# First stage of a two-layer diffusion backbone in another order: modulation blocks ahead of the token tiles' norms

## The chip, the cores and the metric

The program runs on one core of a Trainium2 chip. The metric is the device time of one execution in microseconds (us); the figure compared is the median over runs. The engines are TensorE (PE; PEld is its weight load), VectorE (DVE), ScalarE (ACT), GpSimd (POOL) and SyncE (SP), which issues nearly all transfers here. Each engine works through its own instructions strictly in the order in which they are written, and starts one when the semaphores it names have arrived.

## What is computed

```python
def layer(x, cond, s0_h, s0_r, pos, p):
    mod = jax.nn.silu(cond) @ p["ada_w"] + p["ada_b"]
    sh_m, sc_m, g_m, sh_f, sc_f, g_f = ...            # six vectors of 1024
    h = rmsnorm(x, p["norm_mix"]) * (1.0 + sc_m) + sh_m
    y, S_a, S_b = token_mixers(h, p, s0_h, s0_r, pos)  # h @ w_in, recurrences, @ w_out
    x = x + g_m * y
    h = rmsnorm(x, p["norm_ffn"]) * (1.0 + sc_f) + sh_f
    gate, up = jnp.split(h @ p["w_up"], 2, axis=-1)
    return x + g_f * ((jax.nn.silu(gate) * up) @ p["w_down"]), S_a, S_b
```

Two such layers run over 128 context tokens (condition `c_ctx`) and 512 latent tokens (condition `c`), all in float32, and a last norm follows. Matters here: before the first product with `w_in`, the first layer's scale and shift (2048 of the 6144 columns of `ada_w`) have to be known, and the five tiles of 128 tokens normed.

## The kernel before

The 640 tokens are five tiles `t` of 128 (tile 0 is the context). Products with big weights are made in split passes: an operand `f` is cut into `hi = fp32r(f)` (a cast on ACT) and `lo = f - hi` (a subtraction on DVE), and PE sums hi\*hi + hi\*lo + lo\*hi. The weights come through `Stream` (`W`): `load` issues a transfer of 512 KB on SP's queue, `cut` (L75 on ACT, L76 on DVE) makes `wh` and `wl`. Four `wh`/`wl` pairs and three `raw` buffers exist.

The first stage is `ada_first` (L318 on). It is written under a manual schedule: each engine's order is the order of the calls. Its pieces:

- Block `i` (0 to 3) is 512 columns of `ada_w`: 0 and 1 are the scale and the shift of features 0 to 511, 2 and 3 those of features 512 to 1023. `load(i)` issues four transfers of 512 KB (quarters `j`). `cut(i, j)` makes a quarter's hi (L343, ACT) and lo (L344, DVE). `mm(i, j0, j1)` multiplies quarters with the two silu'd conditions: for blocks in `FAST` four matmuls of 512 columns a quarter, hi and lo alternating (L354), for the others plain float32 matmuls (L357), which need no cut. After quarter 3 ACT copies the sum out (`row`, L362). `rt(i)` turns it into columns (L368, four small matmuls in eight passes), and `fin(i)` adds the bias (L375, DVE; L378 for scales).
- Token tile `t`: `sq` sums squares (L548, ACT; then `rstd`: L559 on DVE and a power on POOL, L561), `xs` scales (L387, DVE), `tr` transposes eight 128x128 squares on PE (L567) and `xc` copies them out (L394, ACT). `full(t, hf)` applies scale and shift to half `hf` of the features, two squares on DVE (L409) and two on ACT (L407), except that `kd=4` puts all on DVE; `split(t, hf)` makes hi (L413, ACT) and lo (L414, DVE) in `hT`.
- The list `out` mixes such calls with entries `(u, hf, k0, k1)`: unit `u` (zf, zb, qa of the first head) for features `k0` to `k1` in eighths, and token half `hf`: 0 is tiles 0 and 1 (256 columns), 1 the other three (384 columns). An entry is 12 matmuls (L605 to L607). The six entries with `4, 8` need the features of blocks 2 and 3; they end the stage. They start with tiles 0 and 1, then go on to the others.
- `setup_lb` (L227 on) computes, from `cols`, the lower bounds of the gates: three small DVE operations, a power of 16 columns on POOL (L236), and eleven small DVE operations (`setup_lb2`). The gates that ACT evaluates when a unit is done (L698) need it.

After the stage the rest of the two layers follows: PE works through `w_in`, `w_out`, `w_up` and `w_down`, while lanes of other work (scans, later modulation, tables) are stepped in between by a count of written-out costs.

Of the kernel before, what the change touches and what calls it, by code (L numbers as in the profile page):

```python
# [20 lines left out]
NT = 5  # L21
# [20 lines left out]
ACC1 = -25.0  # L42
Q_TAB = 2.6
KD = 2
FAST = (0, 1, 3)
CUT = 256
Q_SCAN = 2.65
Q_ADA = (3.0, 2.0, 4.0)
# [54 lines left out]
class Net:  # L103
# [217 lines left out]
    def ada_first(self):  # L321
# [4 lines left out]
        def load(i):  # L326
            col = (1 - i % 2) * 1024 + (i // 2) * 512
            for j in range(4):
                w = self.B("adw")
                nc.sync.dma_start(out=w[:, :1024].rearrange("p (k n) -> p k n", k=2),  # L330
                                  in_=a["ada_w"][0, 2 * j * P:(2 * j + 2) * P, col:col + 512].rearrange(
                                      "(k p) n -> p k n", p=P))
                raws.append(w)
        pr, pc, row, cuts = {}, {}, {}, {}

        def cut(i, j):
            w = raws[4 * i + j]
            if i < 2 or j == 2:
                hi, lo = self.whp.tile([P, 1024], F32R, tag="wh", name="ahi"), \
                    self.wlp.tile([P, 1024], F32R, tag="wl", name="alo")  # L340
            else:
                hi, lo = self.ON("ahi", F32R)[:, :1024], self.ON("alo", F32R)[:, :1024]
            nc.scalar.copy(hi, w[:, :1024])  # L343
            V.tensor_tensor(lo, w[:, :1024], hi.bitcast(F32), op=ALU.subtract)  # L344
            cuts[i, j] = hi, lo

        def mm(i, j0, j1):
            if j0 == 0:
                pr[i] = self.ps("pr")
            for k in range(2 * j0, 2 * j1):  # L350
                sl = slice(k % 2 * 512, k % 2 * 512 + 512)
                if i in FAST:
                    for n, wv in enumerate(cuts[i, k // 2]):
                        nc.tensor.matmul(pr[i][:, :512], self.srv[:, k], wv[:, sl],  # L354
                                         start=k == 0 and n == 0, stop=k == KT - 1 and n == 1)
                else:
                    nc.tensor.matmul(pr[i][:2, :512], self.sT[:, :, k], raws[4 * i + k // 2][:, sl],  # L357
                                     start=k == 0, stop=k == KT - 1)
            if j1 == 4:
                nr = 4 if i in FAST else 2  # L360
                row[i] = self.adp.tile([P, 512], F32, tag="ad", name="row")
                nc.scalar.copy(row[i][:nr, :512], pr[i][:nr, :512])  # L362
# [18 lines left out]
        def sq(t):  # L381
            xn[t] = self.ON("xn")
            self.sq(t, 0, DM, 0, xn[t])
            rs[t] = self.rstd(t, 1)
# [4 lines left out]
        def tr(t):  # L389
            xt[t] = self.norm_b(t, xn[t])  # L390
# [20 lines left out]
        def split(t, hf):  # L411
            f, hi, lo = views(t, hf)
            nc.scalar.copy(hi, f)  # L413
            V.tensor_tensor(lo, f, hi.bitcast(F32), op=ALU.subtract)  # L414

        load(0)
        for t in range(NT):
            self.load_x(t)
        load(1)
        for _ in range(3):  # L420
            self.W.load()
        load(2)
        self.new_hT()
        for j in range(4):
            cut(0, j)
            if j == 3:
                sq(0)
            mm(0, j, j + 1)
        xs(0)
        sq(1)  # L430
        tr(0)
        xs(1)
        sq(2)
        xc(0)
        tr(1)
        xs(2)
        sq(3)
        xc(1)
        tr(2)
        xs(3)  # L440
        sq(4)
        xc(2)
        tr(3)
        self.setup_cols()
        rt(0)
        fin(0)
        cut(1, 0)
        mm(1, 0, 1)
        xs(4)
        xc(3)  # L450
        cut(1, 1)
        tr(4)
        mm(1, 1, 2)
        cut(1, 2)
        xc(4)
        cut(1, 3)
        mm(1, 2, 3)
        self.W.cut()
        mm(1, 3, 4)
        self.W.cut()  # L460
        load(3)
        nc.sync.dma_start(out=self.mask, in_=a["mask"].rearrange("p (b s) -> p b s", b=5))
        nc.sync.dma_start(out=self.rope, in_=a["rope"].rearrange("p (b s) -> p b s", b=2))
        rt(1)
        fin(1)
        mm(2, 0, 2)
        full(0, 0)
        full(1, 0, 4)
        split(0, 0)
        split(1, 0)  # L470
        for t in range(2, NT):
            full(t, 0)
            if t > 2:
                split(t - 1, 0)
        self.W.cut()
        split(4, 0)
        lb = self.setup_lb()
        cut(3, 0)
        cut(3, 1)
        out = [(0, 0, 0, 4), lambda: mm(2, 2, 4), (1, 0, 0, 4), lambda: rt(2), lambda: fin(2),  # L480
               lambda: cut(3, 2), (0, 1, 0, 4), lambda: mm(3, 0, 2), lambda: cut(3, 3), lb, (1, 1, 0, 4),
               lambda: mm(3, 2, 4), lambda: rt(3), lambda: fin(3), (2, 0, 0, 4), (2, 1, 0, 4)]
        for t in range(NT):
            out.append(lambda t=t: full(t, 1, 4 if t == 1 else KD))
            if t:
                out.append(lambda t=t: split(t - 1, 1))
        out.append(lambda: split(NT - 1, 1))
        out += [(u, hf, 4, 8) for hf in range(2) for u in range(3)]
        out.append(self.W.pump)
        return out  # L490

# [770 lines left out]
```

## Time and profile before

| | us |
|---|---|
| median of 3 runs | 1847.48 |
| lowest and highest run | 1845.55 and 1848.51 |
| the profiled execution | 1845.44 |
| its span, first to last instruction | 1843.7 |
| PE busy in the span | 1799.8 (98%) |
| DVE busy, ACT busy | 1062.0 (58%), 710.6 (39%) |
| first stage: first `gw` matmul to the first one after the stage | 36.34 to 69.00 |

Rows of a timeline read: start, duration, engine, line, operation, result <- operands, shapes, and in brackets how long the engine had been idle and what ended it. Durations of neighbours on one engine overlap a little, since an instruction is counted until its last write; the distance from start to start is what a queue pays. "PEclk" or the clock column is the granted TensorE clock: 1.00 is 2.4 GHz and 0.50 is 1.2 GHz.

### The profile page before, as it was taken

To read this page: it belongs to the slowest core of one execution; us is meant where nothing else is said; L and a number is where in the kernel's file an instruction comes from. 1 tells how busy PE (TensorE), PEld (TensorE's weight loads), DVE (VectorE), ACT (ScalarE), POOL (GpSimd) and SP (SyncE) were. 2 spreads that over 40 slices of the span, in tenths; PEclk is the share of its full clock that TensorE was granted. 3 is DMA by queue.
4 is the path that set the end of the run, shared out by engine and by line. 5 is a ranking of instruction groups with operands and counts; after the bars stand their busy time and mean duration, and the time that the engine had idled before them with its cause. 6 is when DMAs were issued, how large, how long until landed. Compare 5 with 4: busy or idle time off the path is not lost.

```text
span 1843.7 us, 29613 instructions
## 1 busy us (share of the span) xinstructions
PE 1799.8 (98%) x12397; PEld 1726.6 (94%) x12397; DVE 1062.0 (58%) x1626; ACT 710.6 (39%) x1207; POOL 51.7 (3%) x59
## 2 busy tenths in 40 slices
PE   7999999999999999999979999999999999999998
PEld 4999999999999989999879999999899998899988
DVE  6797958855755456455566656587475522323234
ACT  7676445543422212222246555455352221122221
POOL 2000000000000000000000000000000000000000
PEclk9999999999999999999989999999999999999999
DMA  9233333221533344343222121322234322222221
GB/s 331 82 102 109 93 120 109 84 78 53 166 117 106 104 132 139 104 123 121 86 92 72 50 69 53 109 78 89 80 92 126 115 75 75 80 81 69 75 75 58
DMA packets 211239, 183.04 MB, mean 99 GB/s; under 512 B 7473, under 2 KB 173073, under 8 KB 211105
## 3 DMA queue, kind: packets, MB, share of 16 engines
q1 hardware_dynamic: 206208, 178.62, 31.0%
q10 hardware_dynamic: 4640, 2.43, 0.4%
q8 instruction: 97, 1.59, 0.4%
q0 software_dynamic: 256, 0.09, 0.1%
q14 instruction: 38, 0.30, 0.0%
HBM read 176.39 MB, written 4.72 MB: 98 GB/s over the span
## 4 chain that ended last, share of the span: by engine, by line
PE 84%; DVE 7%; ACT 4%; DMA 2%; issue 2%; POOL 1%; SPq 0%; DVEq 0%; POOLq 0%; ACTq 0%
PE gw L615 40%; PE ga L1034 5%; PE ga L1036 5%; PE ga L1035 5%; PE ga L661 4%; PE ga L660 4%; PE ga L659 4%; PE pl L752 3%; DMA adw<-in_ada_w 1%; PE gw L606 1%; PE gw L605 1%; PE gw L607 1%; DVE acc L504 1%; DVE wl L76 1%; ACT wh L75 1%
## 5 line engine op out<-in xcount | busy, mean ns | idle before, releaser
L615 PE MATMUL gw<-hT,wh 128*128 128x320 f32 x3712 | 702.1, 310 | 0.2 <-DVE QS L711 0.2
L615 PEld LDWEIGHTS gw<-hT,wh 128*128 128x128 f32 x3712 | 581.3, 188 | 1.5 <-PE pav L880 0.4
L75 ACT CAST wh<-raw 128x1024 fp32r<-128x1024 f32 (+2 forms) x224 | 231.8, 1035 | 701.2 <-PE gw L615 263.8
L76 DVE TENSOR_TENSOR wl<-raw,wh 128x1024 fp32r<-128x1024 f32 (+2 forms) x224 | 269.1, 1204 | 338.8 <-ACT wh L75 338.6
L615 PE MATMUL gw<-hT,wl 128*128 128x320 f32 x1856 | 423.9, 309 | 0.0
L615 PEld LDWEIGHTS gw<-hT,wl 128*128 128x128 f32 x1856 | 310.2, 188 | 0.1
L504 DVE SCALAR_TENSOR_TENSOR acc<-adw,sTt,acc 128x512 f32<-128x512 f32 x280 | 199.2, 747 | 73.6 <-DMA adw<-in_ada_w 73.1
L659 PE MATMUL ga<-wh,hT 128*128 128x256 f32 x640 | 185.6, 290 | 0.0
L661 PE MATMUL ga<-wh,hT 128*128 128x256 f32 x640 | 181.2, 283 | 0.0
L660 PE MATMUL ga<-wl,hT 128*128 128x256 f32 x640 | 181.1, 283 | 0.0
L1034 PE MATMUL ga<-wh,act 128*128 128x512 f32 x330 | 129.6, 393 | 0.0
L1035 PE MATMUL ga<-wl,act 128*128 128x512 f32 x330 | 128.5, 389 | 0.0
L1036 PE MATMUL ga<-wh,act 128*128 128x512 f32 x330 | 127.9, 389 | 0.0
L659 PEld LDWEIGHTS ga<-wh,hT 128*128 128x128 f32 x640 | 122.5, 191 | 0.2
L660 PEld LDWEIGHTS ga<-wl,hT 128*128 128x128 f32 x640 | 122.5, 191 | 0.3
L661 PEld LDWEIGHTS ga<-wh,hT 128*128 128x128 f32 x640 | 122.3, 191 | 0.0
L1085 DVE TENSOR_TENSOR sgf<-sgf,gw 128x640 f32<-128x640 f32 x44 | 36.1, 819 | 141.4 <-PE gw L615 141.2
L1034 PEld LDWEIGHTS ga<-wh,act 128*128 128x128 f32 x330 | 61.9, 188 | 14.1 <-DVE xa L977 1.7
L752 PE MATMUL pl<-X 128*128 128x128 f32 x560 | 72.7, 277 | 1.9 <-ACT X L739 1.7
L1036 PEld LDWEIGHTS ga<-wh,act 128*128 128x128 f32 x330 | 61.9, 188 | 13.0
L1035 PEld LDWEIGHTS ga<-wl,act 128*128 128x128 f32 x330 | 62.0, 188 | 12.4
L752 PEld LDWEIGHTS pl<-X 128*128 128x128 f32 x560 | 67.8, 191 | 4.4 <-ACT X L739 3.8
(225 smaller groups left out, 2603.0 us busy)
## 6 DMA issues: line engine op xcount, KB each, us to landing
raw<-in_w_up SPq DMA_DIRECT2D x88, 512.0 KB, 3.8
adw<-in_ada_w SPq DMA_DIRECT2D x160, 256.0 KB, 2.9
raw<-in_w_in SPq DMA_DIRECT2D x72, 512.0 KB, 3.7
raw<-in_w_down SPq DMA_DIRECT2D x38, 512.0 KB, 3.7
adw<-in_ada_w SPq DMA_DIRECT2D x16, 512.0 KB, 7.5
raw<-in_w_out SPq DMA_DIRECT2D x16, 512.0 KB, 3.9
gate<-in_ada_b SPq DMA_DIRECT2D x8, 512.0 KB, 4.6
x<-in_x_sample SPq DMA_DIRECT2D x4, 512.0 KB, 11.2
```

What stands on the lines that cost most here:

```text
L75: nc.scalar.copy(hi[:, :n], raw[:, :n])
L76: nc.vector.tensor_tensor(lo[:, :n], raw[:, :n], hi[:, :n].bitcast(F32), op=ALU.subtract)
L504: nc.vector.scalar_tensor_tensor(d, w, s, d, op0=ALU.mult, op1=ALU.add)
L615: mm(o, w[:, k], self.hT[:, d, k, sl], start=k == 0 and i == 0, stop=k == KT - 1 and i == 2)
L659: mm(o, a_hi, hi[:, j], start=i == 0, stop=False)
L660: mm(o, a_hi, lo[:, j], start=False, stop=False)
L661: mm(o, a_lo, hi[:, j], start=False, stop=i == nk - 1)
L752: nc.tensor.matmul(pl[:, i * P:(i + 1) * P], X[:, TOK + i * P:TOK + (i + 1) * P], X[:, i * P:(i + 1) * P], start=True, stop=True)
L1034: mm(o, a_hi, hi[:, j], start=i == 0, stop=False)
L1035: mm(o, a_hi, lo[:, j], start=False, stop=False)
L1036: mm(o, a_lo, hi[:, j], start=False, stop=i == nk - 1)
L1085: nc.vector.tensor_tensor(fv.rearrange("p (a b) -> p a b", a=2), sg[:, :TOK].rearrange("p (a b) -> p a b", a=2), ps, op=ALU.mult)
```

## The change

`FAST` takes in block 2, so that it too is multiplied in split passes; its cuts alternate between the `wh`/`wl` buffers (j even) and a wider pool (j odd). The calls of the first stage stand in another order: SP loads block 1 after two token tiles instead of five, and the `w_in` slots lie among the later tiles; blocks 0 and 1 are finished (`fin(1)`), and tiles 0 and 1 split, before tiles 2 to 4 are transposed; those tiles, and all of blocks 2 and 3, move into `out`, among the first entries. `setup_lb` moves from the middle to the end, its second half ahead of the last three entries. What comes after the stage stands in the same order on every engine.

```diff
-FAST = (0, 1, 3)
+FAST = (0, 1, 2, 3)
...
-            if i < 2 or j == 2:
+            if i < 2 or j % 2 == 0:
...
+        def feed(i, j):
+            cut(i, j)
+            mm(i, j, j + 1)
+
         load(0)
-        for t in range(NT):
-            self.load_x(t)
+        self.load_x(0)
+        self.load_x(1)
         load(1)
-        for _ in range(3):
-            self.W.load()
+        self.W.load()
+        self.load_x(2)
+        self.load_x(3)
+        self.W.load()
+        self.load_x(4)
         load(2)
         self.new_hT()
         for j in range(4):
-            cut(0, j)
-            if j == 3:
-                sq(0)
-            mm(0, j, j + 1)
+            feed(0, j)
+        sq(0)
+        self.setup_cols()
+        rt(0)
+        fin(0)
         xs(0)
         sq(1)
         tr(0)
         xs(1)
-        sq(2)
+        feed(1, 0)
         xc(0)
         tr(1)
+        feed(1, 1)
+        xc(1)
+        feed(1, 2)
+        cut(1, 3)
+        self.W.cut()
+        mm(1, 3, 4)
+        sq(2)
+        rt(1)
+        fin(1)
+        full(0, 0)
+        full(1, 0)
+        split(0, 0)
         xs(2)
+        split(1, 0)
+        tr(2)
         sq(3)
-        xc(1)
-        tr(2)
+        self.W.cut()
         xs(3)
-        sq(4)
         xc(2)
         tr(3)
...
+        sq(4)
         load(3)
+        self.W.load()
...
-        rt(1)
-        fin(1)
-        mm(2, 0, 2)
-        full(0, 0)
-        full(1, 0, 4)
-        split(0, 0)
-        split(1, 0)
...
-        lb = self.setup_lb()
-        cut(3, 0)
-        cut(3, 1)
-        out = [(0, 0, 0, 4), lambda: mm(2, 2, 4), (1, 0, 0, 4), lambda: rt(2), lambda: fin(2),
-               lambda: cut(3, 2), (0, 1, 0, 4), lambda: mm(3, 0, 2), lambda: cut(3, 3), lb, (1, 1, 0, 4),
-               lambda: mm(3, 2, 4), lambda: rt(3), lambda: fin(3), (2, 0, 0, 4), (2, 1, 0, 4)]
+        lbs = []
+        out = [(0, 0, 0, 4), lambda: full(2, 0), lambda: xs(4), lambda: xc(3), (1, 0, 0, 4), lambda: tr(4),
+               lambda: split(2, 0), lambda: full(3, 0), lambda: cut(2, 0), lambda: split(3, 0), lambda: xc(4),
+               lambda: mm(2, 0, 1), lambda: full(4, 0), lambda: split(4, 0), lambda: feed(2, 1),
+               (0, 1, 0, 4), lambda: feed(2, 2), lambda: cut(2, 3), (1, 1, 0, 4), lambda: mm(2, 3, 4),
+               lambda: cut(3, 0), lambda: rt(2), lambda: fin(2), lambda: mm(3, 0, 1), lambda: feed(3, 1),
+               lambda: feed(3, 2), self.W.cut, lambda: feed(3, 3), (2, 0, 0, 4), lambda: rt(3), lambda: fin(3),
+               (2, 1, 0, 4)]
...
         out.append(lambda: split(NT - 1, 1))
+        out.append(lambda: lbs.append(self.setup_lb()))
         out += [(u, hf, 4, 8) for hf in range(2) for u in range(3)]
+        out.insert(-3, lambda: lbs[0]())
         out.append(self.W.pump)
```

Three places show what this does to an engine's order. The first is ACT from the moment block 0 is cut (names with numbers are buffers: `xn` squares, `xt` transposed tiles, `ahi` cut quarters). Before:

```order
L548 ACTIVATE xn_197,ssq_101<-x_87 128x1024
L362 COPY row_207<-pr_172 4x512
L548 ACTIVATE xn_210,ssq_101<-x_87 128x1024
L548 ACTIVATE xn_226,ssq_101<-x_87 128x1024
L394 COPY xt_232<-pt_216 128x1024
L548 ACTIVATE xn_244,ssq_101<-x_87 128x1024
L394 COPY xt_250<-pt_234 128x1024
L548 ACTIVATE xn_262,ssq_101<-x_87 128x1024
L394 COPY xt_268<-pt_252 128x1024
L343 CAST ahi_291<-adw_145 128x1024
```

And after (lines behind L470 are four lower):

```order
L362 COPY row_199<-pr_170 4x512
L544 ACTIVATE xn_201,ssq_101<-x_87 128x1024
L544 ACTIVATE xn_220,ssq_101<-x_87 128x1024
L343 CAST ahi_236<-adw_142 128x1024
L394 COPY xt_245<-pt_226 128x1024
L343 CAST ahi_256<-adw_144 128x1024
L394 COPY xt_264<-pt_247 128x1024
L343 CAST ahi_266<-adw_146 128x1024
L343 CAST ahi_274<-adw_148 128x1024
L75 CAST wh_278<-raw_150 128x1024
L362 COPY row_286<-pr_240 4x512
```

The first cut of block 1 moves ahead of three squares and two copies; two of block 1's cuts stand behind a copy that waits for PE.

The second place is ACT at blocks 2 and 3, up to the copy of block 3's row. Before (`row_439` is block 2, `row_523` block 3, `adw_348` to `adw_354` the quarters of block 3):

```order
L343 CAST ahi_410<-adw_348 128x1024
L343 CAST ahi_414<-adw_350 128x1024
L362 COPY row_439<-pr_364 2x512
L343 CAST ahi_461<-adw_352 128x1024
L343 CAST ahi_486<-adw_354 128x1024
L362 COPY row_523<-pr_477 4x512
```

And after (`adw_159` to `adw_163` are quarters 1 to 3 of block 2, `adw_350` to `adw_356` block 3, `wh_515` is the third `w_in` slot):

```order
L343 CAST ahi_433<-adw_159 128x1024
L343 CAST ahi_453<-adw_161 128x1024
L343 CAST ahi_461<-adw_163 128x1024
L362 COPY row_481<-pr_422 4x512
L343 CAST ahi_483<-adw_350 128x1024
L343 CAST ahi_499<-adw_352 128x1024
L343 CAST ahi_507<-adw_354 128x1024
L75 CAST wh_515<-raw_358 128x1024
L343 CAST ahi_519<-adw_356 128x1024
L362 COPY row_527<-pr_494 4x512
```

All four cuts of block 3 and one slot of `w_in` now stand behind the copy of block 2's row, where two stood ahead of it.

The third place is DVE, from block 3's lo halves on. Before, `fin(2)` (two small operations) stood between pairs; after, it reads:

```order
L344 TENSOR_TENSOR alo_484<-adw_350,ahi_483 128x1024
L375 TENSOR_TENSOR modc_102<-pc_487,adab_95 128x2x4
L378 SCALAR_TENSOR_TENSOR modc_102<-modc_102,cols_94 128x2x4
L344 TENSOR_TENSOR alo_500<-adw_352,ahi_499 128x1024
L344 TENSOR_TENSOR alo_508<-adw_354,ahi_507 128x1024
L76 TENSOR_TENSOR wl_516<-raw_358,wh_515 128x1024
L344 TENSOR_TENSOR alo_520<-adw_356,ahi_519 128x1024
L375 TENSOR_TENSOR modc_102<-pc_542,adab_95 128x2x4
```

The four lo halves of block 3, the slot's lo half and both finishes form one run on DVE, and each waits for ACT's cut of the same piece.

## Rows read from the trace of the kernel before

**Rows 1.** The page's engine totals; the trace's stretches (PE, PEld, DVE, ACT, POOL; clock, DMA)

```profile
PE 1799.8 (98%) x12397; PEld 1726.6 (94%) x12397; DVE 1062.0 (58%) x1626; ACT 710.6 (39%) x1207; POOL 51.7 (3%) x59
...
40.00:50.00 10.00, 10.00 (x53) 7.66 (x51) 7.29 (x12) 5.47 (x7) 3.82 (x1) 1.00 0.61 194
...
69.00:1843.70 1774.70, 1744.44 (x12115) 1684.26 (x12114) 1020.88 (x1539) 664.77 (x1139) 39.40 (x37) 1.00 0.30 94
```

**Rows 2.** Timeline of PE in the first stage

```profile
25.78 1.03 PE L567 MATMUL pt<-ident,xn 128*128 128x128 f32 x8
...
30.12 0.50 PE L354 MATMUL pr<-alo,sr 128*128 128x512 f32 x1 [0.76 <-DVE alo L344]
...
30.70 0.39 PE L354 MATMUL pr<-alo,sr 128*128 128x512 f32 x1
31.75 1.05 PE L368 MATMUL pc<-sel,row 4*128 4x2 f32 x8 [0.66 <-ACT row L362]
32.73 3.60 PE L357 MATMUL pr<-adw,sTt 128*2 128x512 f32 x8
36.34 0.39 PE L605 MATMUL gw<-hT,wh 128*128 128x256 f32 x1
...
58.45 0.39 PE L606 MATMUL gw<-hT,wh 128*128 128x256 f32 x1
...
62.75 0.34 PE L605 MATMUL gw<-hT,wh 128*128 128x384 f32 x1
...
69.00 0.28 PE L659 MATMUL ga<-wh,hT 128*128 128x256 f32 x1
```

**Rows 3.** Issues on SP, one for each stretch, with the time to landing

```profile
x<-in_x_sample SPq DMA_DIRECT2D x1, 512.0 KB, 10.2
...
adw<-in_ada_w SPq DMA_DIRECT2D x1, 512.0 KB, 12.5
```

**Rows 4.** Timeline of ACT in the first stage

```profile
14.51 1.05 ACT L548 ACTIVATE xn<-x 128x1024 f32<-128x1024 f32 x1
...
31.12 0.57 ACT L362 COPY row<-pr 4x512 f32<-4x512 f32 x1 [1.36 <-PE pr L354]
...
41.01 2.00 ACT L343 CAST ahi<-adw 128x1024 fp32r<-128x1024 f32 x2
...
56.28 0.88 ACT L407 ACTIVATE xt<-xt,modc 128x128 f32<-128x128 f32 x2
57.07 0.61 ACT L413 CAST hT<-xt 128x512 fp32r<-128x512 f32 x1
...
68.41 0.92 ACT L698 ACTIVATE F<-F,lbc,oml 128x640 f32<-128x640 f32 x1
```

**Rows 5.** Timeline of DVE in the first stage

```profile
33.82 0.16 DVE L375 TENSOR_TENSOR modc<-pc,adab 128x8 f32<-128x8 f32 x1
...
42.72 2.38 DVE L344 TENSOR_TENSOR alo<-adw,ahi 128x1024 fp32r<-128x1024 f32 x2
...
54.64 0.17 DVE L375 TENSOR_TENSOR modc<-pc,adab 128x8 f32<-128x8 f32 x1 [2.76 <-PE pc L368]
```

**Rows 6.** Stretches of PE alone: busy, granted clock, DMA share, GB/s; then its timeline

```profile
19.00:20.00 1.00, 1.00 (x7) 0.50 1.05 387
...
15.89 1.09 PE L567 MATMUL pt<-ident,xn 128*128 128x128 f32 x8 [2.57 <-DVE ms L559]
...
931.23 1.97 PE L516 MATMUL pc<-ident,acc 128*128 128x128 f32 x8 [9.87 <-DVE acc L504]
...
933.43 0.41 PE L661 MATMUL ga<-wh,act 128*128 128x256 f32 x1
933.64 0.41 PE L659 MATMUL ga<-wh,act 128*128 128x256 f32 x1
```

**Rows 7.** Timeline of POOL: the two powers of 16 columns

```profile
42.88 3.82 POOL L236 TENSOR_TENSOR e<-ep,d 128x16 f32<-128x16 f32 x1 [20.51 <-DVE d L234]
...
88.73 5.63 POOL L267 TENSOR_TENSOR u<-ep,na 128x16 f32<-128x16 f32 x1 [33.79 <-DVE na L265]
```

More of the change, by code (lines that the diff above doesn't have):

```diff
@@ L432, in ada_first @@
         xs(1)
-        sq(2)
+        feed(1, 0)
         xc(0)
         tr(1)
+        feed(1, 1)
[10 more added lines that the diff above has]
+        split(0, 0)
         xs(2)
+        split(1, 0)
+        tr(2)
         sq(3)
-        xc(1)
-        tr(2)
+        self.W.cut()
         xs(3)
-        sq(4)
         xc(2)
         tr(3)
-        self.setup_cols()
@@ L445, in ada_first @@
[L445 to L460, printed above, removed]
+        sq(4)
         load(3)
+        self.W.load()
         nc.sync.dma_start(out=self.mask, in_=a["mask"].rearrange("p (b s) -> p b s", b=5))
         nc.sync.dma_start(out=self.rope, in_=a["rope"].rearrange("p (b s) -> p b s", b=2))
-        rt(1)
@@ L465, in ada_first @@
-        fin(1)
-        mm(2, 0, 2)
-        full(0, 0)
-        full(1, 0, 4)
-        split(0, 0)
-        split(1, 0)
[L471 to L476, printed above, removed]
-        lb = self.setup_lb()
-        cut(3, 0)
-        cut(3, 1)
-        out = [(0, 0, 0, 4), lambda: mm(2, 2, 4), (1, 0, 0, 4), lambda: rt(2), lambda: fin(2),
-               lambda: cut(3, 2), (0, 1, 0, 4), lambda: mm(3, 0, 2), lambda: cut(3, 3), lb, (1, 1, 0, 4),
-               lambda: mm(3, 2, 4), lambda: rt(3), lambda: fin(3), (2, 0, 0, 4), (2, 1, 0, 4)]
+        lbs = []
```

## The prediction, made before the changed kernel was run

> **What bounds the kernel now.** I read the page's totals, then the stretches, then PE's timeline in the first stage, then the waits of PE behind it. PE is busy for 1799.8 of 1843.7 us, and of the 1774.7 us behind the stage it is busy for 1744.4, while DVE and ACT are far from full [rows 1]. Since everything behind the stage stands in the same order as before, only the time at which PE leaves the stage can change: 69.00 us, the start of the first L659 [rows 2]. From 36.34 us on PE hardly waits (40 to 50 us: all of it busy [rows 1]); before that it is fed in small pieces. So the change can gain by starting the `gw` matmuls earlier or by taking work off PE, and it loses whatever PE waits after that start.
>
> **Transfers.** They move, but from about 16 us on they set nothing. The first sample tile landed at 4.05 + 10.2 = 14.3 us and block 1's first quarter, four transfers behind it, at 6.95 + 12.5 = 19.5 us [rows 3]: 1.3 us each. With block 1 right behind that tile, its quarters land at about 15.6, 16.9, 18.3 and 19.6 us, and the five tiles and slots and block 2 that follow are all there by about 33 us, block 3 by about 39 us. Below, each is wanted later than that. Its queue is no longer held up by a wait for block 2's float32 products either.
>
> **The steps, first at the full clock.** Prices, start to start where the queue is full: a cut on ACT 0.96 (two in 2.00, each 1.04 long), a square 1.05 and some 0.1 more until its sum is out, a row copy 0.57, two scaled squares 0.88, a hi half 0.6 [rows 4]; a lo half of a quarter 1.19 on DVE [rows 5]; on PE a transposed tile 1.03, 0.95 of it until the next can start, the last three matmuls of a quarter 0.97 behind its lo half, `rt` 1.05, a float32 pair of quarters 3.60, an entry of 256 columns 1.43 and one of 384 columns 2.08 (36 in 58.45 to 62.75 and 36 in 62.75 to 69.00) [rows 2].
>
> 1. To `fin(1)`. The head is as before until PE ends block 0 at 13.3. ACT: row to 13.9, squares of tiles 0 and 1 to 16.1, first cut to 17.1. DVE: `fin(0)` and tile 0 scaled at 16.9, tile 1 at 18.6 (POOL's power lies between), lo half to 19.8. PE: tile 0 to 17.9, block 1's first quarter to 20.8, tile 1 to 21.75. ACT, which takes these in turn: copy to 18.95, cut to 19.9, copy from 21.8 to 22.8, cuts to 24.7. DVE's last lo half ends at 26.1, PE at 27.1, row 27.7, `rt` 28.8, and `fin(1)` at 29.1, behind the `rstd` of tile 2. It was at 33.8 [rows 5]: 4.7 us earlier.
>
> 2. To the first `gw`. Both `full` (four squares an engine) take ACT to 30.9, both hi halves to 32.0, then come tile 3's square (33.05) and the second slot's cut (34.05). On DVE tile 2 is scaled at 32.85, tile 1's lo half ends at 33.45, the slot's lo half at 35.3, tile 3 is scaled at 36.0. On PE the transposes of tiles 2 and 3 stand ahead of the first `gw`: it starts at 37.0, against 36.34 [rows 2]. **What `fin(1)` won is gone here.**
>
> 3. To the end of block 2. PE takes two entries to 40.0 and tile 4 to 41.0. ACT cuts block 2's first quarter at 40.4, splits tile 3 at 40.95, copies tile 4 (42.0), applies and splits it (43.45), and only then cuts quarters 1 to 3 (44.4, 45.3, 46.3); their lo halves are ready at 45.65, 46.8, 47.95. PE has quarter 0 done at 42.7 and waits for quarter 1 until 45.7. Then it goes through: quarter, entry, quarter, entry, quarter, to 52.8. Block 2 costs PE 3.7 us instead of 7.2 (two float32 pairs), and ACT four cuts and DVE four lo halves more.
>
> 4. To the first `4, 8` entry. Block 2's row is out at 53.4, and only now can ACT cut block 3: 54.4, 55.35, 56.3, the slot, the last quarter. DVE has them as one run from 54.4: four lo halves, the slot's, `fin(2)`, 6.2 us in all, to 60.65. PE, with 3.7 us of matmuls and one `rt` to do, is done at 61.65. Before, this block's cuts lay beside entries and float32 work. Then an entry (63.1), `rt(3)` (64.1) and only one entry, 2.08 us, to cover the way from `fin(3)` to tile 1's lo half: that took from 54.64 on DVE to 58.45 on PE, 3.8 us [rows 2, 5]. PE waits 1.7 us, to 67.9.
>
> 5. The last six entries take 10.55 us as before (58.45 to 69.00), so the stage ends at 78.45: **9.45 us later**. As a cross-check, PE's work from 37.0 on is 21.1 for twelve entries, 7.4 for two blocks, 2.1 for two `rt`, 0.95 for tile 4, 31.5 in all, and its waits are 0.7 + 3.0 + 4.4 + 1.7 = 9.8: 78.3.
>
> `setup_lb` at the end: tile 4 is split at 71.2, the three operations end at 71.6, POOL's power takes 3.82 [rows 7], the rest 1.85; the bounds are there at 77.4, and ACT wants them at about 77.9 (L698 came at 68.41, 9.96 us behind the start of the last six entries [rows 4]). DVE holds the next slot's lo half (1.2) behind them, until 78.6, just when PE wants it. I cost that at nothing; the cover is half a microsecond. If the power takes 5.63 us, as its twin did while DVE was full [rows 7], PE waits 1.9 us more. By the Trainium skill's page "SBUF — State Buffer" (section "SBUF: two separate sides") GpSimd and VectorE exclude each other on a shared pair of ports; by that rule the short price holds here, because DVE sits waiting for this very power, and the sum stays as it is. The two rows differ in that sense, though they don't show the cause.
>
> **The clock.** PE stood for 2.57 us after block 0, up to 15.89, and soon ran at 1.2 GHz (19 to 20 us: 0.50); the 9.87 us wait late in the run was followed by slow matmuls too [rows 6]. Eight transposes then take 1.97 us instead of 1.03, and a matmul of 256 columns 0.21 (933.43 to 933.64) instead of 0.119, a factor of 1.8 [rows 2, 6]. The new order has four stretches with as long a wait: 13.3 to 17 and thin work behind it, 28.8 to 32.9, 42.7 to 45.7, and 52.8 to 61.65. At the low level step 1 grows by up to 1.75 (tiles 0 and 1, two quarters' ends), step 2 and the two entries by up to 3.3, step 3's entry by up to 1.7, step 4's and 5's by up to 2.6: 9.4 at most, 0 at least. I take 1.2 + 1.5 + 1.4 = 4.1, nearer to the rows behind 15.89, where the low level ended after a few microseconds of dense work (40 to 50 us: 1.00 [rows 1]). The Trainium skill's page "TensorE: Matmul & The Clock Gate" (section "HAM oscillation — how this bites in real kernels") states the rule behind such a stretch and speaks against this order: waits between bursts make each burst start slow again. Here the rows at 19 and 933 us agree with it.
>
> **The forecast** is 9.45 + 4.1 = 13.55 us later. Made against the profiled execution (1845.44 us, a span of 1843.7 and 1.7 around it) that is 1859.0; that execution lies 2.0 us below the median of the runs shown, so for a median I say 1847.48 + 13.5 = **1861.0 us**.
>
> **Rivals.**
> - The clock holds. Waits of 0.76 and 0.66 us between thin work at 30 to 32 us left the matmuls of 512 columns at 0.39 to 0.50 us [rows 2], the full level's length, and the new waits hold a few matmuls each. Then 9.45 remain: 1857.
> - The late power: 1.9 us on top, 1863, if L236 takes more than about 4.3 us.
> - PE stays fed, the other side. The mechanism: from the first `gw` on PE has 3.5 us less to do in block 2, and if ACT has the quarters of blocks 2 and 3 cut before PE comes to them, the stage ends when PE's 31.5 us are over: 37.0 + 31.5 = 68.5, or 65.0 if tile 3's scaling slips ahead of the second slot and PE starts at 33.5. That is 0.5 to 4 us faster, about 1845. It decides from the point at which quarter 1 of block 2 is cut before 41 us and block 3 before 53 us. Against it stands the order: four of block 3's cuts are behind a copy that waits for PE itself.
> - Lost in a later wait. PE stands 9.9 us once for the modulation lane (9.87 us [rows 6]); if that lane's transfers and sums didn't shift with the stage, 9.9 of 13.5 would go there: 1851. Against it: that lane's steps stand at fixed places among PE's and DVE's work, so it shifts as a whole.
>
> **Chances.** Forecast 0.66, clock holds 0.14, late power 0.06, lost later 0.06, PE fed 0.08. The steps may be off by 3 us either way; with that the forecast's case reaches from 1854 to 1868, the clock rival down to 1853 and the lost one to 1850. The range 1852 to 1868 leaves out the fed PE, most of the lost case and the tails, under 0.2. A measurement tells about 0.2% (3.7 us) from no change. Slower by more than that: 0.66 + 0.14 + 0.06 and half of the lost case, 0.89. Within it: the other half and most of the fed case, 0.08. Faster: 0.03.
>
> **What would show it.** In the changed profile `fin(1)` (L375 the second time) near 29 to 31 us; the first `gw` no earlier than 36; PE idle before block 2's second lo quarter for 2 to 4 us; the copy L362 of block 2's row after 52 us with block 3's casts right behind it, all idle till then; PE busy under 60% between there and the next entry; the last six entries starting at 68 us or later, and from the first L659 on the old distances. Clock rows of 0.50 between 17 and 40 us or behind 45 us make up the second term. If block 3's cuts run beside entries, or the first `gw` comes before 34 us, step 2 or 4 is wrong.

## The result, and the profile after

| | before | after |
|---|---|---|
| median | 1846.76 (4 runs) | 1861.00 (4 runs) |
| lowest and highest | 1845.55 to 1848.51 | 1859.96 to 1861.98 |
| profiled execution, span | 1845.44, 1843.7 | 1859.96, 1858.2 |
| PE busy | 1799.8 | 1802.9 |
| first `gw` to the end of the stage | 36.34 to 69.00 | 38.66 to 82.90 |

The change makes the kernel slower, by 0.75%: the ratio is 1.0075, with a 95% interval of 1.0062 to 1.0088. 1861.0 us had been predicted, in a range of 1852 to 1868.

The page's totals and the stretch behind the stage tell where it went. Columns as in [rows 1].

```profile
PE 1802.9 (97%) x12397; PEld 1732.6 (93%) x12397; DVE 1066.0 (57%) x1628; ACT 714.9 (38%) x1213; POOL 50.8 (3%) x59
...
82.90:1858.20 1775.30, 1744.27 (x12115) 1684.25 (x12114) 1021.05 (x1540) 664.28 (x1139) 39.36 (x37) 1.00 0.30 94
```

Behind the stage hardly anything has changed: 1775.3 us with 1744.27 of PE's work, where there were 1774.7 and 1744.44 [rows 1]. The stage ends 13.90 us later, the span is 14.5 us longer. PE has about as much work in all (1802.9 against 1799.8, low clock included) and more waits.

PE's timeline in the stage, with the waits in brackets (lines behind L470 are four lower than in [rows 2]):

```profile
28.99 1.05 PE L368 MATMUL pc<-sel,row 4*128 4x2 f32 x8 [0.66 <-ACT row L362]
34.03 1.94 PE L563 MATMUL pt<-ident,xn 128*128 128x128 f32 x8 [3.99 <-DVE xn L387]
37.07 1.94 PE L563 MATMUL pt<-ident,xn 128*128 128x128 f32 x8 [1.10 <-DVE xn L387]
38.66 0.56 PE L601 MATMUL gw<-hT,wh 128*128 128x256 f32 x1
...
47.73 0.50 PE L354 MATMUL pr<-ahi,sr 128*128 128x512 f32 x1 [2.68 <-ACT ahi L343]
48.99 0.80 PE L354 MATMUL pr<-alo,sr 128*128 128x512 f32 x1 [0.76 <-DVE alo L344]
...
58.11 1.05 PE L368 MATMUL pc<-sel,row 4*128 4x2 f32 x8 [0.66 <-ACT row L362]
60.32 0.50 PE L354 MATMUL pr<-alo,sr 128*128 128x512 f32 x1 [0.72 <-DVE alo L344]
61.74 0.50 PE L354 MATMUL pr<-alo,sr 128*128 128x512 f32 x1 [0.23 <-DVE alo L344]
65.14 0.50 PE L354 MATMUL pr<-alo,sr 128*128 128x512 f32 x1 [1.08 <-DVE alo L344]
67.46 1.05 PE L368 MATMUL pc<-sel,row 4*128 4x2 f32 x8
71.63 0.39 PE L601 MATMUL gw<-hT,wh 128*128 128x256 f32 x1 [0.81 <-ACT hT L413]
72.35 0.39 PE L602 MATMUL gw<-hT,wh 128*128 128x256 f32 x1 [0.34 <-DVE hT L414]
82.90 0.28 PE L655 MATMUL ga<-wh,hT 128*128 128x256 f32 x1
```

and `fin(1)` in DVE's timeline:

```profile
30.09 0.16 DVE L375 TENSOR_TENSOR modc<-pc,adab 128x8 f32<-128x8 f32 x1
```

`rt(1)` comes 2.8 us earlier than at 31.75 [rows 2] and `fin(1)` 3.7 us earlier than at 33.82 [rows 5], but the first `gw` 2.3 us later: tiles 2 and 3 stand between, and PE waits 3.99 and 1.10 us for DVE to scale them. Then come the waits for block 2's quarter 1 and for block 3. Behind 72.35 all is as before: 10.55 us to the end of the stage.

ACT shows why block 3 is late. In its timeline the copy of block 2's row stands ahead of the casts of block 3:

```profile
46.63 2.93 ACT L343 CAST ahi<-adw 128x1024 fp32r<-128x1024 f32 x3
57.49 0.57 ACT L362 COPY row<-pr 4x512 f32<-4x512 f32 x1 [7.92 <-PE pr L354]
57.97 2.94 ACT L343 CAST ahi<-adw 128x1024 fp32r<-128x1024 f32 x3
61.09 1.05 ACT L75 CAST wh<-raw 128x1024 fp32r<-128x1024 f32 x1 [0.18 <-PE pr L354]
```

ACT is idle for 7.92 us because the copy waits for PE, and the casts, whose data have long been there (from 46 to 65 us the trace shows no transfer at all), go off only behind it. Before, two of them ran ahead of that copy, from 41.01 on [rows 4], and the other two beside entries.

The granted clock, from windows of the trace (length, busy time of PE, PEld, DVE, ACT, POOL, then the clock, the DMA share and GB/s):

```profile
17.00:25.00 8.00, 6.40 (x25) 4.75 (x25) 3.18 (x4) 4.17 (x6) 0.55 (x1) 0.57 1.09 355
...
33.00:37.00 4.00, 1.94 (x8) 1.57 (x8) 3.44 (x6) 2.99 (x6) 0.55 (x1) 0.50 1.07 369
37.00:41.00 4.00, 3.93 (x19) 3.96 (x20) 1.81 (x5) 3.79 (x9) 0.55 (x1) 0.50 1.07 362
...
49.00:53.00 4.00, 4.00 (x13) 3.72 (x14) 2.20 (x2) 0.57 (x1) 0.00 (x0) 0.59 0.00 0
53.00:57.00 4.00, 4.00 (x22) 3.74 (x22) 0.00 (x0) 0.00 (x0) 0.00 (x0) 1.00 0.00 0
```

There are three low stretches, each at a wait (their ends are from windows of 1 us): from 18 to 25 us, behind 1.70 us ahead of tile 0's transposes; from 32 to 42, during and behind the 3.99 us; and from 49 to 52, behind the 2.68 us. A transposed tile takes 1.94 us in the second instead of 1.03.

### The profile page after: what moved, and what is told of

Its sections match the earlier page's. It is cut to its first block, busy times and chain, and to the rows that moved or that the text cites. A ratio compares the mean times of both kernels' runs of the same rounds, so it can differ in the third digit from the quotient of the medians.

```text
span 1858.2 us, 29625 instructions
## 1 busy us (share of the span) xinstructions
PE 1802.9 (97%) x12397; PEld 1732.6 (93%) x12397; DVE 1066.0 (57%) x1628; ACT 714.9 (38%) x1213; POOL 50.8 (3%) x59
## 4 chain that ended last, share of the span: by engine, by line
PE 80%; DVE 9%; ACT 3%; issue 2%; DMA 2%; POOL 1%; DVEq 0%; POOLq 0%; ACTq 0%; SPq 0%
PE gw L611 40%; PE ga L1030 5%; PE ga L1032 5%; PE ga L1031 5%; PE ga L657 4%; PE ga L656 4%; PE ga L655 4%; PE pl L748 2%; DMA adw<-in_ada_w 2%; DVE acc L500 2%; DVE wl L76 1%; ACT wh L75 1%; PE gw L602 1%; PE ga L1009 1%; PE ga L1008 1%
```

## Experiments

Each time stands beside runs of the kernel before on the same chip, whose median lay between 1847.5 and 1847.8 us. "Changed kernel" is the one with the whole change; it was run only for the result, beside runs of the kernel before with a median of 1846.76, so that differences to its 1861.00 us carry that 1 us.

### One part alone: the loads

The kernel before, with nothing changed but the order of the transfers on SP.

```diff
-        for t in range(NT):
-            self.load_x(t)
-        load(1)
-        for _ in range(3):
-            self.W.load()
+        self.load_x(0)
+        self.load_x(1)
+        load(1)
+        self.W.load()
+        self.load_x(2)
...
```

> The kernel before with only SP's order of loads from the change (block 1 and a slot of w_in ahead of token tiles 2 to 4). Theory that the steps set the time and transfers only where a queue wants them early: in the old order ACT squares tile 2 third, at 15.6 us, and now that tile lands at about 22.7, tile 4 at about 27; ACT waits there with all behind it, and the stage ends 4 to 7 us later: 1852 us (1850 to 1854). Rival, that early loads of block 1 are what the change gains and that the order of calls loses alone: the time of before or 1 to 2 us less, 1845 to 1847.

Measured: 1855.30 us (1854.27 to 1856.01), ratio 1.0040 (1.0025 to 1.0055). Slower as expected, and by more than the theory's range. The reason is in ACT's timeline of this kernel:

```profile
22.17 1.06 ACT L552 ACTIVATE xn<-x 128x1024 f32<-128x1024 f32 x1 [6.36 <-DMA x<-in_x_sample]
```

and what it leads to in DVE's, at `fin(1)`:

```profile
43.42 0.16 DVE L375 TENSOR_TENSOR modc<-pc,adab 128x8 f32<-128x8 f32 x1
```

The squares of tile 2 stand ahead of block 1's casts in this order; they wait for a tile that now lands later, and `fin(1)` comes at 43.42 instead of 33.82 [rows 5]. So loads and order of calls belong together: the loads alone are a loss.

### One part alone: block 2 in split passes

The kernel before with `FAST = (0, 1, 2, 3)` and the cuts of block 2 where ACT comes to them first.

```diff
-        mm(2, 0, 2)
...
+        cut(2, 0)
+        cut(2, 1)
...
-        out = [(0, 0, 0, 4), lambda: mm(2, 2, 4), (1, 0, 0, 4), ...
+        out = [(0, 0, 0, 4), lambda: mm(2, 0, 2), lambda: cut(2, 2), lambda: cut(2, 3), (1, 0, 0, 4), ...
```

> The kernel before with only block 2 in split passes (its cuts behind the split of tiles 0 and 1, its matmuls among the first entries, block 3's cuts behind them). PE has 3.5 us less to do, ACT and DVE four cuts more each. Theory that ACT and DVE are what is short up to 50 us: PE waits as long as it saved, 1845 to 1849 us. Rival, that PE's work sets the stage's end: 3 to 3.5 us less, 1843.5.

Measured: 1851.08 us (10 runs, 1849.90 to 1853.83), ratio 1.0019 (1.0009 to 1.0028). The rival (a gain) falls, and the time lies 2 us above the theory's range. PE has 3.5 us less to do, but the float32 products had filled the time in which the first features are split:

```profile
37.34 0.58 PE L605 MATMUL gw<-hT,wh 128*128 128x256 f32 x1 [3.55 <-ACT hT L413]
```

Where PE did 3.60 us of float32 work [rows 2], it now waits 3.55 us, and does that work later. That takes back what the split saves, and no more. Most of the rest is the clock, which is low behind this wait (window of the trace, columns as above):

```profile
37.00:41.00 4.00, 3.51 (x13) 3.13 (x14) 3.68 (x6) 3.74 (x7) 0.00 (x0) 0.50 0.15 22
```

The first entry and the first two quarters of block 2 take 3.24 and 3.21 us there (37.34 to 40.58 to 43.79); in the kernel before the entry takes 2.24 (36.34 to 38.58), and two split quarters 1.85 (46.92 to 48.77).

### The clock

The changed kernel with 51 filler matmuls of 512 columns in PE's gaps up to 45 us. They write the unused half of a sum's buffer.

```diff
+        def warm(i, n):
+            for _ in range(n):
+                nc.tensor.matmul(pr[i][:, 512:], self.srv[:, 0], self.sr1, start=True, stop=True)
...
         rt(1)
+        warm(1, 14)
         fin(1)
```

> The changed kernel with 51 more matmuls of 512 columns in PE's gaps of the first stage, into a part of an accumulator that nobody reads, each group a little shorter than its gap. Theory of the clock term (about 4 us of the loss is PE at 1.2 GHz behind long waits): granted clock 1.00 through most of 17 to 53 us and the stage 2.5 to 4.5 us shorter, 1857.5 us. Rival, that the low clock lies beside waits for ACT and DVE and costs nothing: 1861, or 1 to 2 us more for the matmuls that get in the way.

Measured: 1855.98 us (1855.33 to 1858.25), ratio 1.0046 (1.0031 to 1.0061): 5.0 us under the changed kernel's median, and 3.6 us less in the spans of the profiles. The window of the second low stretch now stands at 1.00:

```profile
33.00:37.00 4.00, 3.70 (x23) 3.04 (x24) 3.27 (x8) 3.94 (x8) 0.92 (x2) 1.00 1.06 372
```

and in PE's timeline the transposes of tiles 2 and 3 are short again:

```profile
33.11 1.09 PE L573 MATMUL pt<-ident,xn 128*128 128x128 f32 x8 [0.51 <-DVE xn L388]
36.24 1.06 PE L573 MATMUL pt<-ident,xn 128*128 128x128 f32 x8 [0.20 <-DVE xn L388]
```

Work that produces nothing makes the kernel faster. This shows the clock term and gives a walk at the full clock to be compared with the prediction: the stage ends at 79.24 here, where 78.45 had been worked out. Block 0's `rt`, which no filler precedes, came 0.67 us later in this execution than in the changed kernel's (14.86 against 14.19). PE's timeline:

```profile
14.86 1.05 PE L369 MATMUL pc<-sel,row 4*128 4x2 f32 x8 [0.23 <-ACT row L363]
...
37.06 0.36 PE L611 MATMUL gw<-hT,wh 128*128 128x256 f32 x1
...
79.24 0.28 PE L665 MATMUL ga<-wh,hT 128*128 128x256 f32 x1
```

### Block 3's casts ahead of the row copies

First try: three quarters' casts ahead of block 2's row copy, the last one and the `w_in` slot behind it.

```diff
-               (0, 1, 0, 4), lambda: feed(2, 2), lambda: cut(2, 3), (1, 1, 0, 4), lambda: mm(2, 3, 4),
-               lambda: cut(3, 0), lambda: rt(2), lambda: fin(2), lambda: mm(3, 0, 1), lambda: feed(3, 1),
-               lambda: feed(3, 2), self.W.cut, lambda: feed(3, 3), (2, 0, 0, 4), ...
+               (0, 1, 0, 4), lambda: feed(2, 2), lambda: cut(2, 3), lambda: cut(3, 0), lambda: cut(3, 1),
+               lambda: cut(3, 2), (1, 1, 0, 4), lambda: mm(2, 3, 4),
+               lambda: rt(2), lambda: fin(2), lambda: cut(3, 3), lambda: mm(3, 0, 4),
+               self.W.cut, (2, 0, 0, 4), ...
```

> The changed kernel with block 3's first three quarters cut ahead of block 2's row copy on ACT (and the last one ahead of the slot of w_in). Theory (step 4: the casts wait behind a copy that waits for PE): PE's gaps behind that copy shrink from some 4.4 us to about 1, 1857.8 us (1857 to 1858.8). Rival, that another wait takes their place at once or that the low clock holds PE there: 1860 to 1861.

Measured: 1862.23 us (1861.29 to 1863.72): no gain, if anything a loss. PE did end block 3 some 3 us sooner, and then stood before the slot, whose cast I had put behind block 3's own row copy (PE's timeline of this kernel):

```profile
64.58 0.38 PE L602 MATMUL gw<-hT,wh 128*128 128x256 f32 x1 [1.61 <-ACT wh L75]
65.84 0.53 PE L604 MATMUL gw<-hT,wl 128*128 128x256 f32 x1 [0.76 <-DVE wl L76]
68.22 1.86 PE L368 MATMUL pc<-sel,row 4*128 4x2 f32 x8
```

It is the same fault one block further on, and the 1.86 us of `rt(3)` show the low clock behind it (0.50 from 67 to 75 us). The second try moves the slot's cast ahead of block 3's last matmuls as well:

```diff
-               lambda: rt(2), lambda: fin(2), lambda: cut(3, 3), lambda: mm(3, 0, 4),
-               self.W.cut, (2, 0, 0, 4), ...
+               lambda: rt(2), lambda: fin(2), lambda: mm(3, 0, 1), lambda: cut(3, 3), self.W.cut, lambda: mm(3, 1, 4),
+               (2, 0, 0, 4), ...
```

> Edit: the changed kernel with three of block 3's cuts ahead of block 2's row copy, and the last one and the third w_in slot's ahead of the matmuls of its last three quarters, so that no cast that PE wants soon stands behind a copy that waits for PE. Theory (step 4 of the prediction: casts behind the row copy): PE's gaps between 57 and 66 us go, the last six entries start 3.2 us earlier than 72.35, and no new wait stands behind block 3's row: 1857.8 (1856.5 to 1859). Rival (the order of the casts is only half of it, since thin work at the low clock fills the time won, as in the run with block 3's quarters alone): 1861 to 1862, with rt(3) at 1.8 us or more and a low clock from 65 to 75 us.

Measured: 1857.82 us (1857.16 to 1859.09), the 3.2 us of the theory. From `rt(2)` on PE no longer waits for a cast (its timeline):

```profile
58.14 1.05 PE L368 MATMUL pc<-sel,row 4*128 4x2 f32 x8 [0.66 <-ACT row L362]
64.40 1.05 PE L368 MATMUL pc<-sel,row 4*128 4x2 f32 x8
```

`rt(3)` follows `rt(2)` by 6.26 us instead of 9.35 (58.11 to 67.46).

### Quarter 1 of block 2 ahead of tile 4

```diff
-               ..., lambda: cut(2, 0), lambda: split(3, 0), lambda: xc(4),
-               lambda: mm(2, 0, 1), lambda: full(4, 0), lambda: split(4, 0), lambda: feed(2, 1),
+               ..., lambda: cut(2, 0), lambda: split(3, 0), lambda: cut(2, 1), lambda: xc(4),
+               lambda: mm(2, 0, 1), lambda: full(4, 0), lambda: split(4, 0), lambda: mm(2, 1, 2),
```

> Edit: the changed kernel with the cut of block 2's quarter 1 ahead of tile 4's copy on ACT, where ACT stands idle, instead of behind tile 4's copy, scaling and splitting. Theory (step 3: quarters 1 to 3 come late because of tile 4's work): PE's waits of 2.68 and 0.76 us ahead of quarter 1 at 47.7 to 49.0 us fall to under 1 in all, block 2 ends 2.5 to 4 us earlier than 57.45 and the stage with it: 1858 (1857 to 1859). Rival (quarter 2 or tile 4's halves wait in its place, or the cut itself only shifts the wait to tile 4): block 2 ends within 1 us of 57.45, and 1861.

Measured: 1857.73 us (1856.21 to 1858.14), 3.3 us less than the changed kernel, as the theory had it. Ahead of block 2's second quarter PE waits under 0.3 us now, and 0.8 us for tile 4 behind it (its timeline):

```profile
48.49 0.44 PE L601 MATMUL gw<-hT,wh 128*128 128x384 f32 x1 [0.51 <-ACT hT L413]
49.22 0.44 PE L602 MATMUL gw<-hT,wh 128*128 128x384 f32 x1 [0.29 <-DVE hT L414]
```

### Tile 3 behind the first entry

```diff
-        tr(3)
...
-        out = [(0, 0, 0, 4), lambda: full(2, 0), ...
+        out = [(0, 0, 0, 4), lambda: tr(3), lambda: full(2, 0), ...
```

> Edit: the changed kernel with the transposes of tile 3 moved from ahead of the first entry to behind it. The step behind it: the squares of tiles 2 and 3 are what starts the first gw at 38.7 us in the changed kernel, though hT of tiles 0 and 1 is ready earlier; PE stands before tile 3's transposes (37.07) for DVE to scale it. Theory: first gw about 2.0 to 2.5 us earlier (36.2 to 36.7), and what is won is kept as far as PE's next wait (for block 2's quarter 1) doesn't take it: 1859 (1858 to 1861). Rival: PE comes earlier to the same quarter 1, whose cut stands behind tile 4's work on ACT, waits as much longer there and the end stays: 1861.

Measured: 1861.08 us (1859.47 to 1863.09): the rival holds. The first `gw` comes 7.44 us behind `rt(1)` instead of 9.67, and all of it is lost again, because tile 3 is now late on ACT and every cast of block 2 stands behind it. PE's timeline:

```profile
30.88 1.86 PE L368 MATMUL pc<-sel,row 4*128 4x2 f32 x8 [0.67 <-ACT row L362]
...
38.32 0.56 PE L600 MATMUL gw<-hT,wh 128*128 128x256 f32 x1
...
45.77 0.49 PE L354 MATMUL pr<-ahi,sr 128*128 128x512 f32 x1 [1.04 <-ACT ahi L343]
...
50.63 0.79 PE L354 MATMUL pr<-ahi,sr 128*128 128x512 f32 x1 [2.65 <-ACT ahi L343]
```

So the place where the prediction has the gain go is real, but not the last one: behind it ACT's queue decides.

### All of them, and fillers

The last three edits together, 33 fillers ahead of the first entry, and the entry of unit 2 for tiles 0 and 1 behind `fin(3)`.

```diff
-               ..., self.W.cut, lambda: mm(3, 1, 4), (2, 0, 0, 4), lambda: rt(3), lambda: fin(3),
+               ..., self.W.cut, lambda: mm(3, 1, 4), lambda: rt(3), lambda: fin(3), (2, 0, 0, 4),
                (2, 1, 0, 4)]
```

> Edit: the three other edits of this group together (tile 3's transposes behind the first entry, quarter 1 of block 2 ahead of tile 4's copy, block 3's cuts ahead of the copies), filler matmuls that keep PE's clock up in its first gaps, and the entry of unit 2 for tiles 0 and 1 behind fin(3), where it covers the split of block 3's features. Theory (the three places and the clock make up the loss between them, and the order of the first stage can't be better than PE's own work from the first gw on): the sum of parts is -2 -3.2 -3 -3.6, of which some overlap: 1851 (1850 to 1854), still not below the kernel before. Rival (the change is good in itself and lost only by these placements): below 1846, faster than before. Second rival (the waits only move from one place to the next): 1856 or more, no better than the fillers alone.

Measured: 1854.17 us (5 runs, 1852.44 to 1858.37), ratio 1.0039 (1.0025 to 1.0053). It lies just above the first theory's range; the rival (the change is good, only badly placed) falls as far as these edits go. Against the fillers alone (1.0046, 1.0031 to 1.0061) the runs show no clear gain, so that the second rival is not excluded by the times. In its profile the stage ends at 75.32, 3.9 us ahead of the run with fillers and 6.3 us behind the kernel before. Two low stretches are left: one from 29 to 33 us slows the 14 fillers behind `rt(1)` (5.08 us instead of 3.47), and tile 2's transposes, ready a microsecond earlier, start only behind them; the other, from 43 to 50 us, comes with waits of 1.07, 0.76 and 0.52 us for quarters of block 2. Another 3.2 us go behind the stage, where no instruction changed place. The largest single part is the wait for the modulation lane, which had lasted 9.87 us [rows 6] and takes 1.4 us more (view: waits of PE):

```profile
PE pc L521 <- DVE acc L509: 11.3, 1, 11.3
```

### Block 2 in float32

```diff
-FAST = (0, 1, 2, 3)
+FAST = (0, 1, 3)
...
-               ..., lambda: cut(2, 0), ..., lambda: feed(2, 1),
-               (0, 1, 0, 4), lambda: feed(2, 2), lambda: cut(2, 3), (1, 1, 0, 4), lambda: mm(2, 3, 4),
+               ..., lambda: mm(2, 1, 2),
+               (0, 1, 0, 4), lambda: mm(2, 2, 3), (1, 1, 0, 4), lambda: mm(2, 3, 4),
```

> Edit: the changed kernel with block 2 back in float32 products (no cuts, twice the time on PE), all else in its order. Theory: in this order splitting block 2 is itself a loss, since its 3.5 us less on PE are bought with four cuts and four lo halves that PE then waits for (2.68 + 0.76 us at quarter 1) and with the low clock behind those waits; without the split PE goes through at the full clock and block 2 ends about 2 us earlier than 57.45, block 3's part stays as it is: 1858.5 (1857 to 1860). Rival (the split saves PE time as meant, and the loss is all in the order): 3.5 us more, 1864.

Measured: 1861.38 us (1859.87 to 1862.59). Neither: in this order the split is worth nothing that the runs can tell (1861.38 against 1861.00). PE does 3.6 us of float32 products at a stretch where it had waited 2.68 + 0.76 us, and the copy of block 2's row, here in ACT's timeline, comes 28.8 us behind `rt(1)`, where it was 28.5.

```profile
59.44 0.57 ACT L362 COPY row<-pr 2x512 f32<-2x512 f32 x1 [8.90 <-PE pr L357]
```

Block 3's casts still stand behind it.

### The early finish, with float32 work as cover

The changed kernel's loads and its order up to `fin(1)`, but block 2 in float32: two quarters where PE waits behind `rt(1)`, two ahead of the third entry.

```diff
         rt(1)
         fin(1)
+        mm(2, 0, 2)
...
+        out = [(0, 0, 0, 4), lambda: tr(2), lambda: xc(2), lambda: xs(4), (1, 0, 0, 4), lambda: full(2, 0),
+               lambda: split(2, 0), lambda: tr(3), lambda: xc(3), lambda: tr(4), lambda: full(3, 0),
+               lambda: xc(4), lambda: split(3, 0), lambda: full(4, 0), lambda: split(4, 0), lambda: cut(3, 0),
+               lambda: cut(3, 1), lambda: mm(2, 2, 4), (0, 1, 0, 4), lambda: cut(3, 2), lambda: cut(3, 3),
+               lambda: rt(2), lambda: fin(2), lambda: mm(3, 0, 4), self.W.cut, (1, 1, 0, 4), lambda: rt(3), lambda: fin(3),
+               (2, 0, 0, 4), (2, 1, 0, 4)]
```

> Edit: the changed kernel's loads and its early fin(1), but block 2 in float32 products, half of them where PE waits behind rt(1) and half ahead of the third entry; tiles 2 to 4 transposed between entries; block 3 cut while those run, its finish ahead of the last two entries. Theory (PE's own work bounds the stage wherever PE stays fed; the early fin(1) is worth only what PE can do with it): by adding up, rt(1) at 28, then 37.25 us of the work that stood between rt(1) and the stage's end in the kernel before, 2.9 us for three transposed tiles that now come later: the stage ends at 68 instead of 69.0, so 1846.5 (1844 to 1849), no measurable difference from the kernel before. Rival (early loads of block 1 and late token tiles are a loss in themselves, as the run with the loads alone might say): 1850 or more. Second rival (the early finish pays): below 1843.

Measured: 1848.93 us (11 runs, 1846.76 to 1852.04), ratio 1.0009 (1.0000 to 1.0018): 12 us of the 14 are back. PE's timeline of this kernel:

```profile
29.00 1.05 PE L368 MATMUL pc<-sel,row 4*128 4x2 f32 x8 [0.66 <-ACT row L362]
29.98 3.60 PE L357 MATMUL pr<-adw,sTt 128*2 128x512 f32 x8
...
40.67 1.09 PE L560 MATMUL pt<-ident,xn 128*128 128x128 f32 x8 [1.35 <-ACT xt L394]
...
70.91 0.28 PE L652 MATMUL ga<-wh,hT 128*128 128x256 f32 x1
```

The early loads and late token tiles are no loss in themselves beyond the 0.1% of this ratio. Of the 2.9 us by which the stage ends behind the 68 worked out, 1.0 is `rt(1)`, at 29.00 instead of 28. The waits behind it (0.66, 1.35, 0.37 and 0.29 us) add up to 2.67, where the 37.25 us taken over from the kernel before held 1.00 (0.34 and 0.66 us of waits in its trace); this difference is most of the rest. The last run goes at these waits, with scale and shift of tiles 2 to 4 on DVE alone, and puts in 19 fillers before `rt(1)`.

```diff
-        xs(2)
         split(1, 0)
+        xs(2)
...
-        ... lambda: full(2, 0), lambda: split(2, 0), lambda: tr(3), lambda: xc(3), lambda: tr(4), lambda: full(3, 0),
+        ... lambda: full(2, 0, 4), lambda: tr(3), lambda: xc(3), lambda: split(2, 0), lambda: tr(4), lambda: full(3, 0, 4),
...
```

> Edit: the kernel of the last run (early fin(1), block 2 in float32) with its remaining waits taken away: scale and shift of tiles 2 to 4 all on DVE, so that ACT copies tiles 3 and 4 sooner (PE waited 1.35 us for that, and 0.37 + 0.29 us for tile 4's halves), tile 1's lo half ahead of tile 2's scaling (0.66 us), and 19 filler matmuls in the gaps before block 1 is done, where the clock was low (rt(1) came at 29.0 instead of 28.15 with fillers). Theory (with all waits gone the stage is PE's own work and lasts as long as before): the stage ends at 70.91 - 2.67 - 0.85 = 67.4 us, 1.6 us ahead of the kernel before: 1846 (1844.5 to 1848), 0.1% faster at most, hardly to be told from no change. Rival (the waits come back elsewhere): 1848 to 1850. Second rival (the early finish pays more than the added transposes cost): below 1843.

Measured: 1847.87 us (11 runs, 1845.85 to 1849.46) beside 1847.81, ratio 0.9999 (0.9990 to 1.0008). No difference from the kernel before: inside the theory's range, at its upper end. The rival's waits came back in part: 2.2 us of them remain in the stage (1.10 for a copy, 0.82 and 0.28 for tile 4's halves), which ends at 69.49, not at 67.4. Behind the stage this profile takes 2.1 us more than the kernel before.

## Why the prediction was right, point by point

- **Step 1, `fin(1)`**: 29.1 at the full clock and 1.2 for the clock. It came at 30.09, and at 29.25 with fillers. Right, though counted from block 0's row the way with fillers was some 0.7 us shorter than worked out (14.72 to 29.25, against 13.9 to 29.1).
- **Step 2, first `gw`**: 37.0 at the full clock, with step 1's 1.2 and a part of the 1.5 that were taken for this step and the two entries behind it: 38.2 to 39.7. It came at 38.66, and at 37.06 with fillers. Right, as was the reason: tiles 2 and 3 stand ahead of it. But moving tile 3 away gave nothing; what is won there is lost again in step 3, which the prediction did not say.
- **Step 3, end of block 2**: 52.8 worked out for the full clock; with fillers the row copy started at 53.82. The wait is where it was put, and one edit takes it away. At the full clock the term was 1 us too small. ACT's copy of tile 4 stood 0.83 us for a buffer that a quarter of block 2 holds until DVE has made its lo half (both come from the same pool); I had missed that release. The rows in ACT's timeline, first of the run with fillers, then of the changed kernel:

```profile
41.94 1.02 ACT L395 COPY xt<-pt 128x1024 f32<-128x1024 f32 x1 [0.83 <-DVE alo L345]
...
44.16 1.01 ACT L394 COPY xt<-pt 128x1024 f32<-128x1024 f32 x1 [1.34 <-PE pt L563]
```

In the changed kernel itself the buffer cost nothing: the low clock made tile 4's transposes late, and the copy waited for those.

- **Step 4, block 3 behind the row copy**: 15.1 us from the end of block 2 (52.8) to the last six entries (67.9). It took 14.9, from 57.45 (the end of the last lo matmul ahead of the copy) to 72.35. By the prediction's prices PE's gaps are 3.9 us there (8.69 us from 57.45 to the row copy at 66.14, less 3.7 of matmuls and 1.05 of `rt`). The prediction's own times give 4.1 in the same way (52.8 to 61.65); its cross-check has 4.4, so its sum is 0.3 too high. At the end the way from the covering entry to the second matmul of the last six is 1.7 us, as worked out, 1.15 of it counted as idle. One sign did not come: PE was to be busy under 60% between the row copy and the next entry, and the profile has 68% (5.80 of 8.49 us), since it counts these matmuls until their end, 0.39 to 0.50 us each, and the prices from start to start, 0.23. The two tries with block 3's casts show the mechanism from both sides.
- **Step 5, the last entries and the bounds**: 10.55 us as before. The bounds cost nothing; the cover was there, for DVE started the next slot's lo half at 80.69 and PE went through at 82.90. The power, in POOL's timeline of the changed kernel, took less than either row of [rows 7]:

```profile
75.98 2.91 POOL L236 TENSOR_TENSOR e<-ep,d 128x16 f32<-128x16 f32 x1 [7.14 <-DVE d L234]
```

- **The clock**: 4.1 us taken. By the profiles with and without fillers it is 3.7 at the stage's end (82.90 and 79.24) and 4.3 counted from block 0's `rt`; by the medians it is 5.0, and 6.0 if each is set against its own runs of the kernel before. Three of the four stretches named ran low. In the fourth, behind 53 us, the clock stood at 1.00: the last 1.4 came to 1.3, all at 49 to 52 us (2.93 us for an entry of 2.08, 1.44 for three matmuls of 0.97). The rule cited in the prediction from the Trainium skill's page "TensorE: Matmul & The Clock Gate" (section "HAM oscillation — how this bites in real kernels"), that waits between bursts make each burst start slow, agrees with the three stretches of the changed kernel and with the run in which fillers close the gaps. Not every wait does it: in the run with the early finish the clock stayed at 1.00 through 1.35 us between dense work.
- **Rivals**: the late power did not come, and the clock did not hold. "PE stays fed" was not built as stated, with split passes and every quarter cut in time. The run with all edits comes nearest and took 1854; the last two feed PE with float32 products, 3.5 us more work, and give the time of the kernel before. Whether the 1845 of that rival can be had stays open. "Lost in a later wait" did not happen in the changed kernel (10.1 us against 9.9). That wait did take some 1.5 us more in the run with all edits and in the last one (11.3 and 11.4 us); why these two is not settled.

The stage ended at 82.90 against 78.45 + 4.1 = 82.55. That it came so near is in part luck: at the full clock the missed buffer adds 1 us and the way to `fin(1)` was 0.7 us shorter than worked out, and in the changed kernel the low clock hides the buffer. That the median came out at 1861.0 to the tenth is chance too: the difference forecast was 13.5 us, and 14.2 were measured by the medians, 14.5 by the spans of the profiles.

## What to carry to other kernels

In this kernel, finishing an input earlier was worth only what the bounding engine could do with it: the early `fin(1)` paid nothing, since the engines that feed PE were then busy with the tiles that had been put off. Before making work shorter on the bounding engine, look at what it covers; float32 products that need no preparation kept PE busy and its clock up, while products of half the length needed casts that were not there in time. On engines with one queue each, look for every copy that waits for the bounding engine, and for the casts behind it that wait for nothing else.

## What the runs showed of the hardware that I had not expected

The 16-column power on POOL took 2.91 us while DVE stood waiting for it, in the changed kernel and in the nine other profiles that have it at the end of the stage. It took 3.82 us in the kernel before and in the two runs that leave it in the middle, with DVE in lo halves, and its twin beside a busy DVE 5.63 us [rows 7]. That is in line with the Trainium skill's page "SBUF — State Buffer" (section "SBUF: two separate sides") on the shared ports; no run here took the cause apart.

The four executions of the changed kernel fall into two pairs, with spans of 1858.2 and 1858.4 and of 1860.1 and 1860.2 us. The profiles without fillers that share its order up to `rt(1)` show it at 28.7 to 29.0 us (four kernels) or at 30.6 to 30.9 (three). In the later ones 0.4 us or more of the delay is there already at block 0's `rt` (14.6 to 15.4 us, against 13.9 to 14.2), and the clock falls a second time at 27 or 28 us, behind waits of 0.8 to 1.1 and of 0.76 us, so that block 1's last matmuls run at 0.63 us instead of 0.40. In the others the first of these waits was 0.34 us and the clock stayed up. So the same order can meet the low clock in one place or in two. That the pairs of spans come from this is argued, since only one execution of each kernel has a trace.
